# The first expert's gather laced into its first chunk, with its low halves on VectorE and six loads ahead in one ring

## The chip, the cores and the metric

The kernel runs on one core of a Trainium2 chip, in one launch. The metric is the device time in microseconds (us) of that core. PE is TensorE, DVE is VectorE, ACT is ScalarE, POOL is GpSimd and SP is SyncE, whose queue issues the loads of the weights here.

## What is computed

A trunk of two decoder layers on 256 tokens of width 1024, in fp32: latent attention and a dense feed-forward block, then a gated delta rule and a block of 8 experts, of which each token uses two. The part that matters here is the experts':

```python
def moe_ffn(h, w_router, w_gate_up, w_down):
    t = h.reshape(B * S, D)
    logits = (t @ w_router).astype(jnp.float32)
    top_val, top_idx = lax.top_k(logits, TOP_K)
    top_w = jax.nn.softmax(top_val, axis=-1)
    combine = jnp.sum(jax.nn.one_hot(top_idx, N_EXPERTS) * top_w[..., None], axis=1)
    out = jnp.zeros((B * S, D), jnp.float32)
    for e in range(N_EXPERTS):
        y_e = swiglu_ffn(t, w_gate_up[e], w_down[e])   # (silu(gate) * up) @ down
        out = out + combine[:, e:e + 1] * y_e
    return out
```

`w_gate_up` is 1024 by 2 x 1408 for each expert, `w_down` 1408 by 1024. `t` is the normalised and modulated state of the 256 tokens.

## The kernel before

**Halves.** A product in fp32 is made of three products of numbers rounded to fp32r: high by high, low by high, high by low. So each slab of weights is split: ACT casts it to the high half `whi` (L199), and another engine subtracts that from the slab to get the low half `wlo` (L200), here DVE, since `pool_share` is 0 in this phase (L1739). The pool `wsp` has four buffers for each half (L59), so at most four split slabs wait for PE.

**Loads.** `wload` (L182) takes a buffer of 512 KB and issues the load on SP. In the experts' phase `in_turn` (L1734) says which ring the buffer is from: `wr2`, six buffers in memory that the phase before gives up when it ends (L1730), or `wrw`, ten buffers that exist all along (L57). Three loads of eight go to `wr2`. The slabs 0 to 3 of expert 0 are loaded and split in the phase before (`tokens`, L1610) and wait in the list `pre`. The list `ahead` (L1753) holds two more loads, of slabs 4 and 5; `routed` (L1764) splits them.

**Routing and gather.** `routed` makes the two weights of each token (it holds an exponential and a switch of ACT's function table, L1772 and L1773, and four small matmuls, L1778, whose result DVE copies, L1779). `place` (L1841) writes a matrix `P` that picks the tokens of an expert. `gather` (L1871) then, after a row of factors `xr`, makes for each of eight blocks `k` of 128 features: four matmuls with `P` (L1901), DVE's scaling `xg` (L1905), ACT's high half `XH` (L1910), and the low half `XL`. For the first group `share` is true: for odd blocks ACT writes a full-precision copy `full` (L1917) and POOL subtracts (L1918); for even blocks DVE does it in one instruction (L1920), one block late.

**The expert.** `expert` (L2057) goes through chunks of 512, 512 and 384 columns of gate and up. For a chunk of 512 it takes eight slabs (L2064); for each, six matmuls (L2069): high by `XH`, low by `XH`, high by `XL`, for two parts of 256 columns each. After slabs 3, 5 and 7 `sides` (L2051) advances side work. For expert 0 that is `first_sides` (L2119): `turns_of` (L1782, 15 small DVE instructions that find the order of the experts), placements for the next group, `weights_of` (L1803, 17 small DVE instructions and one of ACT), then the next group's gather. After the chunk come the gating (`gated`, L2037), the transposes and halves `ah` and `al` (`turned`, L2007), and, a chunk later, the products with `w_down` (`down`, L1973).

**Order.** Inside `manual_schedule` PE, DVE, ACT and POOL run in the order in which the program is written. Outside, a planner lays out the instructions when the program is built. SP's loads are always laid out by the planner. Before, the written order ends after the whole gather and `routed` (`order.close()`, L2136), ahead of expert 0; its chunks and the side work are the planner's.

Of the kernel before, what the change touches and what calls it, by code (L numbers as in the profile page):

```python
# [8 lines left out]
F32 = mybir.dt.float32  # L9
# [3 lines left out]
AF = mybir.ActivationFunctionType  # L13
# [4 lines left out]
S = 256  # L18
# [31 lines left out]
def hybrid_kernel(ctx: ExitStack, tc: tile.TileContext, rope_rows, x, c, positions, ada_w, ada_b,  # L50
# [1682 lines left out]

    def in_turn():  # L1734
        nload[0] += 1
        return wr2 if nload[0] % 8 in (0, 3, 6) else wrw

    ring.append(in_turn)
    pool_share[0] = 0  # L1739
# [10 lines left out]
    nc.gpsimd.tensor_copy(slot2[:, 0:64], slot[:, 0:64])  # L1750
    nc.gpsimd.tensor_copy(slot2[:, 192:256], slot[:, 0:64])

    ahead = [gu_load(0, k0, 0, 512) for k0 in (4, 5)]  # L1753
    cnt, cntm, trank, eidS, cntS = (sm.tile([128, NE], F32, name=n, bufs=1) for n in ("cnt", "cntm", "trank", "eidS", "cntS"))
    tge, perm = (sm.tile([128, NE, NE], F32, name=n, bufs=1) for n in ("tge", "perm"))
    chosS, posS, w2s = rt("chosS"), rt("posS"), rt("w2s", (128, 2, 1))
# [7 lines left out]
    def routed():  # L1764

        mx, w2 = rt("mx", (128, 2, 2)), rt("w2", (128, 2, 1))
        nc.vector.tensor_scalar(oh0, rank, 1.0, None, op0=OP.is_lt)
        nc.vector.reduce_max(mx[:, :, 0:1], lg, axis=AX.X)
        nc.vector.scalar_tensor_tensor(lg, in0=oh0, scalar=-3e38, in1=lg, op0=OP.mult, op1=OP.add)
        nc.vector.reduce_max(mx[:, :, 1:2], lg, axis=AX.X)  # L1770
        nc.vector.tensor_tensor(w2, mx[:, :, 1:2], mx[:, :, 0:1], op=OP.subtract)
        nc.scalar.activation(w2, w2, AF.Exp)  # L1772
        warm(AF.Silu)  # L1773
        for raw in ahead:
            pre.append(wsplit(raw, [128, 1, 2, 512]))
        pt = acc_bank("tot")
        for t in range(2):
            mm(pt[:, 0:NE], lhsT=ones32[:, 0:1].to_broadcast([128, 128]), rhs=chos[:, t], start=t == 0, stop=t == 1)  # L1778
        nc.vector.tensor_copy(cnt, pt[:, 0:NE])  # L1779
        nc.vector.tensor_copy(w2s, w2)  # L1780
# [47 lines left out]
    def experts(again, between):  # L1828
# [39 lines left out]

        XS = {}

        def gather(g, share=False):  # L1871

            es = gathers[g]
            small = [e for e in es if kinds[e] == "S"]
# [22 lines left out]
            for k in range(8):  # L1897
                ps = mm_bank("xg")
                for j, src in enumerate((xtH, xtL)):
                    for t in range(2):  # L1900
                        mm(ps[:, :n], lhsT=src[:, t, k * 128:(k + 1) * 128], rhs=P[:, t, pl],  # L1901
                           start=j == 0 and t == 0, stop=j == 1 and t == 1)
                xg = sm.tile([128, S], F32, name="xg", tag="xg")
                sh = modT[1, 3][:, k:k + 1]
                nc.vector.scalar_tensor_tensor(xg[:, :n], in0=ps[:, :n], scalar=scl[1, 1][:, k:k + 1], in1=xr[:, :n],  # L1905
                                               op0=OP.mult, op1=OP.mult)
                xb = xg[:, bo:bo + 128]
                while late:
                    late.pop()()
                nc.scalar.activation(XH[:, k, :], xb, AF.Identity, bias=sh)  # L1910
                if small:
                    nc.scalar.activation(XF[:, k, :].rearrange("p (a b) -> p a b", b=64),
                                         xg.rearrange("p (a b) -> p a b", b=64)[:, 0:3 * len(small) - 2:3], AF.Identity,
                                         bias=sh)
                if share and k % 2:
                    full = sm.tile([128, S], F32, name="full", tag="act")
                    nc.scalar.activation(full[:, :128], xb, AF.Identity, bias=sh)  # L1917
                    nc.gpsimd.tensor_tensor(XL[:, k, :], full[:, :128], XH[:, k, :].bitcast(F32), op=OP.subtract)  # L1918
                else:
                    late.append(lambda k=k, xb=xb, sh=sh: nc.vector.scalar_tensor_tensor(  # L1920
                        XL[:, k, :], in0=xb, scalar=sh, in1=XH[:, k, :].bitcast(F32), op0=OP.add, op1=OP.subtract))
                if not share or k == 7:
                    while late:
                        late.pop()()
                yield
# [131 lines left out]
        def expert(e, more):  # L2057
            XH, XL = XS[e]
            for c0, n in groups(e):
# [1 line left out]
                ps = [mm_bank("gu") for _ in parts]  # L2061
                kn = 512 // max(n, 256)
                for k0 in range(0, 8, kn):
                    hi, lo = pre.pop(0) if pre else wsplit(gu_load(e, k0, c0, n), [128, kn, 2, n])  # L2064
                    for k in range(kn):
                        kk = k0 + k
                        for i, (w, x) in enumerate(((hi, XH), (lo, XH), (hi, XL))):
                            for p, (o, m) in zip(ps, parts):
                                mm(p[:, :2 * m].rearrange("p (g c) -> p g c", g=2), lhsT=x[:, kk, :],  # L2069
                                   rhs=w[:, k, :, o:o + m], start=kk == i == 0, stop=kk == 7 and i == 2)  # L2070
                    if k0 % 2 and k0 > 1:
                        sides(more)
                for p, (o, m) in zip(ps, parts):
                    act = sm.tile([128, S], F32, name="act", tag="act", bufs=2)
                    gated((p[:, :m], p[:, m:2 * m]), m, act[:, :m])
# [54 lines left out]
        if again:  # L2130
            list(group(0))
        else:
            place(0, pos, chos)
            list(gather(0, True))
            between()
            order.close()  # L2136
        run = {"B": expert, "S": expert_small}
        for e in range(NE):
            more = [group(g) for g, es in enumerate(gathers) if g and e == es[0] - 1]
# [91 lines left out]
```

## Time and profile before

| what | value |
|---|---|
| median of 3 runs | 995.1 us (992.34 to 997.79) |
| the profiled execution: its own time | 997.03 us |
| the profiled execution: its span | 995.3 us |
| PE busy, share of the span | 931.6 us, 94% |
| DVE busy | 671.4 us, 67% |
| ACT busy | 486.2 us, 49% |
| POOL busy | 123.7 us, 12% |

The span goes from the first to the last instruction of the program in one profiled execution; its time includes what lies around the span. Start times in the views are microseconds from the span's start. The shares are means over stages with different limits; the stage of the change lies between 580 and 655 us. A busy time of PE is modelled, and PE's clock has two levels here, shown as a granted share of 0.50 (1.2 GHz) and 1.00 (2.4 GHz); a value between them is a mean over a stretch.

### The profile page before, as it was taken

The page shows a single profiled execution, that of the slowest core. Times are in us where ns is not written, and L with a number is a line of the kernel's source. Part 1 is how long each engine was busy: PE and PEld are TensorE (multiplying, and loading weights), DVE is VectorE, ACT ScalarE, POOL GpSimd, SP SyncE. Part 2 cuts the span into 40 slices and gives each one's busy share as a digit, 9 for nine tenths or more (in the row PEclk, how much of TensorE's full clock was granted, in tenths as well). Part 3 has the DMA queues.
Part 4 walks back from the last instruction along what each step waited for, and adds up shares of the span by engine and source line. Part 5 has one row for each costly group of instructions (what it writes and reads, how often), then busy time and mean ns, then how long its engine had stood idle before and what let it go on. Part 6 is the DMA issues. An engine that isn't in the chain of part 4 may idle for free. (4 is left out here: it accounts for less than half of the span.)

```text
span 995.3 us, 18930 instructions
## 1 busy us (share of the span) xinstructions
PE 931.6 (94%) x6802; PEld 749.5 (75%) x6802; DVE 671.4 (67%) x1281; ACT 486.2 (49%) x877; POOL 123.7 (12%) x226
## 2 busy tenths in 40 slices
PE   5899999999999999899999989899989999999995
PEld 3787888999999989789889877755774567356642
DVE  5778957877777768977764458925872488257532
ACT  2366646444444457544563366723662366236422
POOL 2000001000000024535663240000000000000000
PEclk7999998999999989899999979999999999999998
DMA  9959995979988955432223365979999999999992
GB/s 308 366 178 315 303 288 167 312 238 338 312 285 293 304 163 179 140 107 86 86 86 101 113 212 175 318 259 370 365 394 370 363 353 342 382 358 367 364 372 71
DMA packets 152741, 261.34 MB, mean 263 GB/s; under 512 B 13650, under 2 KB 104832, under 8 KB 152640
## 3 DMA queue, kind: packets, MB, share of 16 engines
q1 hardware_dynamic: 152336, 259.81, 76.3%
q8 instruction: 55, 0.90, 0.4%
q0 software_dynamic: 304, 0.25, 0.1%
q14 instruction: 46, 0.38, 0.1%
HBM read 258.97 MB, written 1.05 MB: 261 GB/s over the span
## 5 line engine op out<-in xcount | busy, mean ns | idle before, releaser
L463 ACT CAST whi<-w 128x1024 fp32r<-128x1024 f32 (+3 forms) x147 | 138.6, 958 | 115.4 <-PE gu L1145 45.0
L200 DVE TENSOR_TENSOR wlo<-w,whi 128x1024 fp32r<-128x1024 f32 (+1 forms) x136 | 153.0, 1155 | 33.8 <-ACT whi L199 32.1
L468 DVE TENSOR_TENSOR wlo<-w,whi 128x1024 fp32r<-128x1024 f32 (+3 forms) x132 | 147.9, 1135 | 21.6 <-ACT whi L463 21.2
L199 ACT CAST whi<-w 128x1024 fp32r<-128x1024 f32 (+1 forms) x136 | 131.8, 998 | 35.7 <-PE gu L2069 18.5
L1144 PE MATMUL gu<-hhi,whi 128*128 128x256 f32 x336 | 95.4, 284 | 0.0
L1146 PE MATMUL gu<-hhi,wlo 128*128 128x256 f32 x336 | 95.1, 283 | 0.0
L1145 PE MATMUL gu<-hlo,whi 128*128 128x256 f32 x336 | 95.1, 283 | 0.0
L2099 PE MATMUL gu<-w,XF 128*64 128x512 f32 (+1 forms) x384 | 85.3, 564 | 0.0
L232 PE MATMUL pj<-hhi,whi 128*128 128x256 f32 x240 | 73.6, 307 | 0.0
L234 PE MATMUL pj<-hhi,wlo 128*128 128x256 f32 x240 | 68.5, 286 | 3.8 <-DVE wlo L468 3.8
L233 PE MATMUL pj<-hlo,whi 128*128 128x256 f32 x240 | 68.4, 285 | 0.0
L468 POOL TENSOR_TENSOR wlo<-w,whi 128x1024 fp32r<-128x1024 f32 x15 | 39.3, 2622 | 226.3 <-DVE al L1119 181.2
L1145 PEld LDWEIGHTS gu<-hlo,whi 128*128 128x128 f32 x336 | 64.5, 192 | 0.0
L1144 PEld LDWEIGHTS gu<-hhi,whi 128*128 128x128 f32 x336 | 64.5, 192 | 0.0
L1146 PEld LDWEIGHTS gu<-hhi,wlo 128*128 128x128 f32 x336 | 64.5, 192 | 0.0
L2069 PE MATMUL gu<-whi,XH 128*128 128x512 f32 x192 | 59.4, 390 | 3.6 <-ACT whi L199 3.4
L2069 PE MATMUL gu<-wlo,XH 128*128 128x512 f32 x192 | 59.7, 392 | 2.2 <-DVE wlo L200 2.2
L2099 PEld LDWEIGHTS gu<-w,XF 128*64 128x64 f32 x384 | 26.4, 136 | 44.5 <-issue 39.5
L2069 PE MATMUL gu<-whi,XL 128*128 128x512 f32 x192 | 58.2, 385 | 0.0
L262 DVE SCALAR_TENSOR_TENSOR adacc<-adaw,csil,adacc 128x1024 f32<-128x1024 f32 x42 | 56.1, 1336 | 2.2 <-DMA adaw<-in_ada_w_dram 2.2
L1106 PE MATMUL acc<-ah,whi 128*128 128x256 f32 x176 | 50.0, 284 | 0.0
L1107 PE MATMUL acc<-al,whi 128*128 128x256 f32 x176 | 49.8, 283 | 0.0
(526 smaller groups left out, 2213.0 us busy)
## 6 DMA issues: line engine op xcount, KB each, us to landing
w<-in_moe_w_down_dram SPq DMA_DIRECT2D x84, 512.0 KB, 6.8
w<-in_moe_w_gate_up_dram SPq DMA_DIRECT2D x128, 256.0 KB, 5.4
w<-in_moe_w_gate_up_dram SPq DMA_DIRECT2D x64, 512.0 KB, 6.9
adaw<-in_ada_w_dram SPq DMA_DIRECT2D x50, 512.0 KB, 5.3
w<-in_moe_w_gate_up_dram SPq DMA_DIRECT2D x128, 192.0 KB, 4.0
w<-in_ada_w_dram SPq DMA_DIRECT2D x46, 512.0 KB, 6.6
w<-in_ffn_w_gate_up_dram SPq DMA_DIRECT2D x88, 256.0 KB, 5.5
w<-in_gdn_w_in_dram SPq DMA_DIRECT2D x32, 512.0 KB, 4.6
```

The source lines that it names most:

```text
L199: nc.scalar.copy(dv(hi), rv(raw))
L200: eng.tensor_tensor(dv(lo), rv(raw), dv(hi).bitcast(F32), op=OP.subtract)
L232: mm(ps, lhsT=lhi, rhs=rhi, start=first, stop=False)
L233: mm(ps, lhsT=lhi, rhs=rlo, start=False, stop=False)
L234: mm(ps, lhsT=llo, rhs=rhi, start=False, stop=last)
L463: nc.scalar.copy(dv(hi), rv(raw))
L468: eng.tensor_tensor(dv(lo), rv(raw), dv(hi).bitcast(F32), op=OP.subtract)
L1144: mm(o, lhsT=h[:, c], rhs=rh, start=k == g == 0 and new, stop=False, skip_group_check=True)
L1145: mm(o, lhsT=h[:, c], rhs=rl, start=False, stop=False, skip_group_check=True)
L1146: mm(o, lhsT=l[:, c], rhs=rh, start=False, stop=k == 1 and g == 3, skip_group_check=True)
L2069: mm(p[:, :2 * m].rearrange("p (g c) -> p g c", g=2), lhsT=x[:, kk, :], rhs=w[:, k, :, o:o + m], start=kk == i == 0, stop=kk == 7 and i == 2)
L2099: mm(o, lhsT=X[:, k, :], rhs=r, start=k == 0, stop=k == 7, tile_position=(0, 64 * h))
```

## The change

The gather of expert 0 becomes a generator `rows0` that is advanced one block at a time. The factors and the blocks 0 and 1 are made ahead of the expert. In its first chunk a function `step(k)` comes ahead of the products of slab k: it makes block k + 2, at slab 2 it also calls `routed` (`between()`), and at slabs 1 to 6 it splits one of the slabs loaded ahead. The low halves `XL` are all made on DVE, one block late; the branch with `full` and POOL goes. `ahead` holds six loads, slabs 4 to 7 and the first two of the second chunk, and the first six loads all take buffers of `wrw`. `routed` no longer splits. The written order ends after the first chunk's products, so that the side work after slabs 3, 5 and 7 stands in it too.

```diff
--- before.py
+++ after.py
@@ -1733,7 +1733,7 @@
 
     def in_turn():
         nload[0] += 1
-        return wr2 if nload[0] % 8 in (0, 3, 6) else wrw
+        return wr2 if nload[0] > 6 and nload[0] % 8 in (0, 3, 6) else wrw
 
     ring.append(in_turn)
     pool_share[0] = 0
@@ -1750,7 +1750,7 @@
     nc.gpsimd.tensor_copy(slot2[:, 0:64], slot[:, 0:64])
     nc.gpsimd.tensor_copy(slot2[:, 192:256], slot[:, 0:64])
 
-    ahead = [gu_load(0, k0, 0, 512) for k0 in (4, 5)]
+    ahead = [gu_load(0, k0, 0, 512) for k0 in (4, 5, 6, 7)] + [gu_load(0, k0, 512, 512) for k0 in (0, 1)]
     cnt, cntm, trank, eidS, cntS = (sm.tile([128, NE], F32, name=n, bufs=1) for n in ("cnt", "cntm", "trank", "eidS", "cntS"))
     tge, perm = (sm.tile([128, NE, NE], F32, name=n, bufs=1) for n in ("tge", "perm"))
     chosS, posS, w2s = rt("chosS"), rt("posS"), rt("w2s", (128, 2, 1))
@@ -1771,8 +1771,6 @@
         nc.vector.tensor_tensor(w2, mx[:, :, 1:2], mx[:, :, 0:1], op=OP.subtract)
         nc.scalar.activation(w2, w2, AF.Exp)
         warm(AF.Silu)
-        for raw in ahead:
-            pre.append(wsplit(raw, [128, 1, 2, 512]))
         pt = acc_bank("tot")
         for t in range(2):
             mm(pt[:, 0:NE], lhsT=ones32[:, 0:1].to_broadcast([128, 128]), rhs=chos[:, t], start=t == 0, stop=t == 1)
@@ -1868,7 +1866,7 @@
 
         XS = {}
 
-        def gather(g, share=False):
+        def gather(g, late_by=0):
 
             es = gathers[g]
             small = [e for e in es if kinds[e] == "S"]
@@ -1912,14 +1910,9 @@
                     nc.scalar.activation(XF[:, k, :].rearrange("p (a b) -> p a b", b=64),
                                          xg.rearrange("p (a b) -> p a b", b=64)[:, 0:3 * len(small) - 2:3], AF.Identity,
                                          bias=sh)
-                if share and k % 2:
-                    full = sm.tile([128, S], F32, name="full", tag="act")
-                    nc.scalar.activation(full[:, :128], xb, AF.Identity, bias=sh)
-                    nc.gpsimd.tensor_tensor(XL[:, k, :], full[:, :128], XH[:, k, :].bitcast(F32), op=OP.subtract)
-                else:
-                    late.append(lambda k=k, xb=xb, sh=sh: nc.vector.scalar_tensor_tensor(
-                        XL[:, k, :], in0=xb, scalar=sh, in1=XH[:, k, :].bitcast(F32), op0=OP.add, op1=OP.subtract))
-                if not share or k == 7:
+                late.append(lambda k=k, xb=xb, sh=sh: nc.vector.scalar_tensor_tensor(
+                    XL[:, k, :], in0=xb, scalar=sh, in1=XH[:, k, :].bitcast(F32), op0=OP.add, op1=OP.subtract))
+                if not late_by or k == 7:
                     while late:
                         late.pop()()
                 yield
@@ -2061,7 +2054,12 @@
                 ps = [mm_bank("gu") for _ in parts]
                 kn = 512 // max(n, 256)
                 for k0 in range(0, 8, kn):
-                    hi, lo = pre.pop(0) if pre else wsplit(gu_load(e, k0, c0, n), [128, kn, 2, n])
+                    if e == c0 == 0 and not again:
+                        step(k0)
+                    if pre:
+                        hi, lo = pre.pop(0)
+                    else:
+                        hi, lo = wsplit(ahead.pop(0) if ahead else gu_load(e, k0, c0, n), [128, kn, 2, n])
                     for k in range(kn):
                         kk = k0 + k
                         for i, (w, x) in enumerate(((hi, XH), (lo, XH), (hi, XL))):
@@ -2070,6 +2068,8 @@
                                    rhs=w[:, k, :, o:o + m], start=kk == i == 0, stop=kk == 7 and i == 2)
                     if k0 % 2 and k0 > 1:
                         sides(more)
+                if e == c0 == 0 and not again:
+                    order.close()
                 for p, (o, m) in zip(ps, parts):
                     act = sm.tile([128, S], F32, name="act", tag="act", bufs=2)
                     gated((p[:, :m], p[:, m:2 * m]), m, act[:, :m])
@@ -2131,9 +2131,18 @@
             list(group(0))
         else:
             place(0, pos, chos)
-            list(gather(0, True))
-            between()
-            order.close()
+            rows0 = gather(0, 1)
+            for _ in range(3):
+                next(rows0)
+
+            def step(k):
+
+                next(rows0, None)
+                if k == 2:
+                    between()
+                if k > 0 and ahead:
+                    pre.append(wsplit(ahead.pop(0), [128, 1, 2, 512]))
+
         run = {"B": expert, "S": expert_small}
         for e in range(NE):
             more = [group(g) for g, es in enumerate(gathers) if g and e == es[0] - 1]
```

## Rows read from the trace of the kernel before

**Rows 1.** Busy time by stage: us, busy of each engine (instructions), PEclk, DMA, GB/s.

```profile
585.60:594.10 8.50, 8.44 (x40) 8.47 (x40) 3.83 (x13) 3.99 (x12) 1.37 (x3) 0.50 0.91 342
594.20:599.90 5.70, 5.70 (x15) 4.44 (x16) 2.26 (x8) 3.50 (x7) 0.46 (x1) 0.50 0.00 0
608.30:614.40 6.10, 4.73 (x24) 3.70 (x24) 6.10 (x30) 4.38 (x9) 0.00 (x0) 1.00 0.37 118
614.40:632.10 17.70, 17.03 (x83) 13.59 (x83) 17.70 (x34) 11.46 (x21) 0.00 (x0) 1.00 0.85 282
646.30:653.60 7.30, 7.30 (x36) 6.03 (x35) 2.16 (x5) 1.51 (x3) 0.00 (x0) 0.90 0.66 219
```

**Rows 2.** Time line of PE: start, us, instructions merged; gather, then expert 0's first chunk.

```profile
586.54 0.63 PE L1901 MATMUL xg<-P,xtH 128*128 128x128 f32 x2
...
587.40 0.63 PE L1901 MATMUL xg<-P,xtH 128*128 128x128 f32 x2
...
594.18 1.20 PE L2069 MATMUL gu<-whi,XH 128*128 128x512 f32 x2
...
596.89 1.05 PE L2069 MATMUL gu<-whi,XH 128*128 128x512 f32 x2
...
599.45 0.87 PE L2069 MATMUL gu<-whi,XH 128*128 128x512 f32 x2
...
601.08 0.63 PE L2069 MATMUL gu<-whi,XH 128*128 128x512 f32 x2
...
607.62 0.63 PE L2069 MATMUL gu<-whi,XL 128*128 128x512 f32 x2
```

**Rows 3.** Time line of DVE in the same stretch and behind it.

```profile
588.49 0.35 DVE L1905 SCALAR_TENSOR_TENSOR xg<-xg,scl,xr 128x128 f32<-128x128 f32 x1 [0.43 <-PE xg L1901]
...
594.21 0.17 DVE L1767 TENSOR_SCALAR oh<-rank 128x16 f32<-128x16 f32 x1
...
600.77 1.22 DVE L200 TENSOR_TENSOR wlo<-w,whi 128x1024 fp32r<-128x1024 f32 x1 [1.34 <-ACT whi L199]
...
603.51 0.17 DVE L1785 COPY cntm<-cnt 128x8 f32<-128x8 f32 x1
...
610.34 0.27 DVE L1762 TENSOR_REDUCE posS<-byt 128x16 f32<-128x128 f32 x1
...
610.66 1.23 DVE L1845 TENSOR_SCALAR P<-slot,posS,chosS 128x256 fp32r<-128x256 f32 x4
...
614.36 4.61 DVE L200 TENSOR_TENSOR wlo<-w,whi 128x1024 fp32r<-128x1024 f32 x4
```

**Rows 4.** Time line of ACT in the same stretch.

```profile
588.88 0.40 ACT L1910 ACTIVATE XH<-xg,mod 128x128 fp32r<-128x128 f32 x1 [0.38 <-DVE xg L1905]
589.18 0.39 ACT L1917 ACTIVATE full<-xg,mod 128x128 f32<-128x128 f32 x1
...
595.55 1.28 ACT L413 ACT_TABLE_LOAD   x1
...
597.13 1.04 ACT L199 CAST whi<-w 128x1024 fp32r<-128x1024 f32 x1
599.69 1.05 ACT L199 CAST whi<-w 128x1024 fp32r<-128x1024 f32 x1 [1.52 <-PE gu L2069]
```

**Rows 5.** Time line of PE, two of its waits behind the first chunk.

```profile
614.34 0.74 PE L2069 MATMUL gu<-wlo,XH 128*128 128x512 f32 x2 [0.69 <-DVE wlo L200]
...
643.19 0.38 PE L1859 MATMUL psw<-cmb,P 128*128 128x2 f32 x2 [2.65 <-ACT SM L1862]
```

**Rows 6.** Groups of DVE from 600 to 632: count, busy us, mean ns, idle before.

```profile
L1845 DVE TENSOR_SCALAR P<-slot,posS,chosS 128x256 fp32r<-128x256 f32 (+1 forms) x14 | 4.6, 367 | 0.0
...
L2039 DVE TENSOR_TENSOR act<-act,gu 128x256 f32<-128x256 f32 x4 | 1.6, 410 | 0.0
```

**Rows 7.** Time line of SP: loads of gate and up, merged.

```profile
536.56 41.55 SPq L185 DMA_DIRECT2D w<-in_moe_w_gate_up_dram  x20
```

**Rows 8.** Page part 6, DMA issues: count, KB each, median us to landing.

```profile
w<-in_moe_w_gate_up_dram SPq DMA_DIRECT2D x128, 256.0 KB, 5.4
```

## The prediction

> **What bounds the kernel now.** I read the page's busy times first, then a table of busy times by stage, then the time lines of TensorE (PE), VectorE (DVE) and ScalarE (ACT) around the edit. PE is the busiest engine there, so in most places the end is moved by PE's own work or by what makes PE stand still. By stage [rows 1] it looks otherwise around the first expert. While the rows of expert 0 are gathered (585.6 to 594.1) and while its first chunk begins (594.2 to 599.9) PE is full, but at a granted clock of 0.50, 1.2 GHz. Behind 600 it has 1.00. From 608.3 to 614.4 DVE is busy 6.10 of 6.10 us, and from 614.4 to 632.1 17.70 of 17.70: there DVE, not PE, is the scarce engine, and PE waits for it where I follow it: 0.69 us for a low half at 614.34 [rows 5]. Only from 646.3 does DVE have room again (2.16 of 7.30 us). So two questions decide: does PE get through gather and first chunk sooner, and does DVE leave that stretch sooner or later?
>
> **What PE could win.** Before, the gather's eight blocks come first, at half clock 0.86 us each (586.54 to 587.40), and the first product of expert 0 starts at 594.18; a slab's six matmuls take 2.56 us at 1.2 GHz (596.89 to 599.45) and 1.40 us at 2.4 (6.54 us for 14 pairs from 601.08 to 607.62); the last pair, with its 0.63, ends at 608.25 [rows 2]. PE never idles in it. The change sets three blocks ahead of product 0 and puts one block before each of the next five. Product 0 then starts at 586.54 + 3 x 0.86 = 589.1, five microseconds sooner. PE's work is the same, matmul for matmul; the gain is only in the clock. Before, it stayed at 0.50 through 8.5 us of gather and the first 5.8 us of products [rows 1, 2]. If it rises as long after the first product as it did here, or somewhat sooner, that is 593 to 595 instead of 600, and 5 to 7 us at half clock become full ones: 2.5 to 3.5 us of PE time.
>
> **What DVE and ACT must do in each step.** This is the part on the path. In the new first chunk all engines follow the written order. In step k, DVE does xg (block k+2), the low half XL of the block before, then wlo of a slab; ACT does XH of block k+2, then whi of that slab. So wlo waits for whi, whi stands behind XH, XH waits for xg, and the next xg stands behind this wlo: one ring over two engines. Its links: xg to XH 0.39 (588.49 to 588.88), XH to ACT's next 0.30 (588.88 to 589.18), whi to wlo 1.08 (599.69 to 600.77), wlo to DVE's next 1.15 (4.61 for four) [rows 3, 4]. Sum 2.92 us per step. At half clock PE needs 0.86 + 2.56 = 3.42 per step and the ring is hidden; at full clock PE needs half of 0.86 and 1.40 = 1.83 and the ring sets the pace. Before, gather and splits were not laced in one another, and from 600 a split every 1.40 us kept up with PE.
>
> Two things are put into that ring. Step 2 holds `between()`: five small DVE instructions, the exponential, and the switch of ACT's table, all before whi. From the first small one to the whi behind the switch it took 594.21 to 597.13 = 2.92 us [rows 3, 4]. With xg and XL before it (0.27 each by their starts) and wlo's 1.08 + 1.15 behind, step 2 is 5.7 us. The table load in it is 1.28 us by its row, and the cast follows it 0.30 us after its end. The Trainium skill, ScalarE: Activation LUTs, "What ACT_TABLE_LOAD costs", gives each switch a further drain of about 1.38 us, 2.66 in all; the rows here show no such drain ahead of it or behind it, and by that figure, an estimate, the end would be 1.4 us later. The sum does not use it. Step 3 is followed by `turns_of`, 15 DVE instructions of about 0.16 to 0.27 us (first and last in [rows 3]); I take 0.19 each by their starts, 2.8 us. Before, the planner laid them between splits that were already ahead; now wlo of the next slab and XL of the next block are queued behind them, and PE's third pair of each slab waits for that XL.
>
> **The sum.** Block 3 ends at 589.1 + 2.56 + 0.86 = 592.5, its xg starts 0.2 later (588.26 to 588.49), 592.8. Step 1 ends at 595.7, step 2 at 601.4, step 3 with `turns_of` at 607.1, step 4 at 610.0. The last two blocks' low halves: XL of block 6 is ready at 610.6, of block 7 at 611.2 (0.39 + 0.40 + 0.34 behind xg). PE finishes slab 6 at 611.1 and slab 7 at 612.5: 4.2 us after the 608.25 of before, with the clock's gain already spent, since PE waits for XL in slabs 4, 5 and 6. DVE goes on: wlo of slab 8 to 612.9, four placements 1.16 (of the row with 1.23) and seven small ones of `weights_of` at 0.16 to 615.2, wlo of slab 9 to 616.3, ten small ones to 617.9, the two gating products 0.8 [rows 6], wlo of slab 10 by 619.8. Before, that one ended at 614.3, where PE had it [rows 5]. So DVE is 5.5 us late at the point where PE already waited for it.
>
> **Does it come back?** From there to 632 DVE has no idle time in which to catch up, so I let the 5.5 us stand. Downwards, the bound is the placements for later groups, 10 of the 14 that DVE did between 600 and 632 (4.6 us for all, so 3.4 after the first four) [rows 6]: nothing soon needs them, and put off to DVE's room after 646 they would give 3.3 back. Upwards, the bound is the two al subtractions coming ahead of wlo 10 with the wait for their transposes, some 1.4 us more. I take 5.5, since the order of the stage stays as it is written.
>
> **The parts at nothing.** Six loads ahead in the ring of ten: the loads of this chunk were issued from 536 on, and from 594.2 to 599.9 the DMA moved 0 GB/s because no buffer was free [rows 1, 7]. So no split of this stretch waits for a landing, and other buffer turns alone win nothing. What is behind them on SP's queue is freed by wlo 4 to 9, at 596 to 616; the DMA share of 0.37 to 0.85 up to 632 is the cover. If it were gone, one split would wait for one landing, 5.4 us by the page's median [rows 8]. Four low halves move from POOL and ACT to DVE: 4 x 0.27 = 1.1 us, which lie where DVE waits for whi in the ring; without that wait they would cost 1.1. The four `full` activations leave ACT (0.39 each), and were off the path.
>
> **From span to time.** The span of the profiled execution is 995.3 and its time 997.03, 1.9 above the median 995.1 of the runs. With 5.5 more, span 1000.8 and time 1002.5 on its terms; set on the median, 995.1 + 5.5 = **1000.6 us**. Behind 660 PE keeps its pace and loads follow freed buffers, so a shift there passes to the end.
>
> **The rivals.**
> - *The forecast* (0.50): the ring over DVE and ACT, 998.5 to 1004.
> - *Late, but worked off* (0.20): the chunk ends 4 us later, the later placements give way, 5.5 - 3.3 = 2.2 remain: 997.3. For it: DVE's room after 646. Against: these placements stood among urgent splits before, too.
> - *The clock wins* (0.15), on the other side: the low halves run far enough ahead (four buffers) that the ring doesn't hold PE, and PE's 2.5 to 3.5 us reach the end: 992.1. It decides if a step of DVE and ACT stays under 1.83 us at full clock; DVE alone is 0.27 + 0.27 + 1.15 = 1.69, so it needs whi not to wait for xg. For it speaks how long the clock lay at 0.50 while PE was full. The Trainium skill, TensorE: Matmul & The Clock Gate, section "What's actually happening", says "the default state is throttled, and activity releases the throttle"; by that, products laced into the gather release it sooner. The trace agrees that it came back after 5.8 us of products, but 8.5 us of gather before them had not brought it back, and no row tells what a mixture does.
> - *Late and throttled again* (0.15): PE idles about 4 us for XL of block 5 and falls to 0.50, as after the idle 2.65 us at 643.19 [rows 5], behind which the clock is 0.90 on the mean from 646.3 [rows 1]. Slab 7 then takes 2.56 instead of 1.40, the al subtractions come first (1.4): 1003.2 and up to 1006.
> - That the loads do not come sooner at all changes nothing, by the paragraph above.
>
> **The numbers.** Range 994 to 1006: it holds the forecast, the second case, the slow end of the clock case and most of the last one, about 0.8. About 0.5% (5 us) is what a measurement can tell from no change. Slower by more: 0.36 of the forecast's 0.50 and the last case's 0.15, 0.51; faster by more needs more than the clock case gives, 0.05; the rest, 0.44, within.
>
> **What would show it.** Right: in the chunk, wlo to wlo about 2.9 us apart and more in steps 2 and 3, ACT idle for xg, PE idle for XL in slabs 4 to 6, the chunk's last pair near 612, wlo 10 near 620. Clock back by 595. Wrong: no idle PE between 589 and 608 and the chunk done by 605 (the clock case), or a chunk end near 612 and expert 1's first product no later than before (worked off). If DVE's small instructions stand elsewhere than after slab 3, the sum's 2.8 goes.

## The result, and the profile after

The changed kernel takes 1003.3 us in the median of 20 runs (998.46 to 1005.84). The kernel before took 996.5 us in the median of 20 runs beside it (991.68 to 997.79). The ratio is 1.0070, with a 95% interval of 1.0059 to 1.0082: 6.8 us are lost, somewhat more than the 5.5 of the forecast.

The profiled execution of the changed kernel took 1000.44 us, its span 998.7. Its gather begins at 584.93, 0.73 us sooner than in the trace of before, since stages in front of the change ran differently; so stretches are compared by their lengths. First the busy times by stage of the changed kernel: gather and first chunk, then to the first product with `w_down`, then about as far again (us, busy of PE, PEld, DVE, ACT and POOL with instructions, granted clock, DMA share, GB/s).

```profile
584.90:612.60 27.70, 22.22 (x88) 17.50 (x88) 17.65 (x56) 10.97 (x19) 0.00 (x0) 0.71 0.47 164
612.60:629.40 16.80, 15.08 (x78) 12.16 (x78) 15.84 (x38) 10.89 (x19) 0.00 (x0) 1.00 0.64 209
629.40:655.10 25.70, 22.30 (x113) 18.31 (x113) 19.86 (x33) 17.64 (x34) 0.00 (x0) 0.93 0.89 313
```

The same view of the kernel before, with the stages cut at the same instructions:

```profile
585.70:608.20 22.50, 22.50 (x88) 19.36 (x88) 13.19 (x38) 13.85 (x24) 1.82 (x4) 0.68 0.58 200
608.20:624.50 16.30, 14.87 (x78) 12.26 (x78) 16.30 (x44) 10.29 (x20) 0.00 (x0) 1.00 0.67 216
624.50:650.10 25.60, 22.23 (x114) 18.28 (x113) 21.77 (x42) 17.19 (x33) 0.00 (x0) 0.93 0.89 313
```

The loss stands in the first row: the same 88 PE instructions take 27.7 us instead of 22.5, and PE, which was full before, is idle for 5.5 of them. The second stage adds 0.5, the third 0.1. From 655 to 900 us each product starts 4.9 to 5.0 us later than its like before, in both kernels' own times (0.73 of the loss is hidden by the earlier gather). Nothing is worked off up to there. Behind 900 the two executions come nearer, to the 3.4 us by which their spans differ, but not by any work of the change: behind a wait that both have, PE's clock fell in the execution of the kernel before (0.57 on the mean from 900 to 904) and stayed at 1.00 in that of the changed kernel. Before, and after:

```profile
899.99 0.94 PE L2069 MATMUL gu<-whi,XH 128*128 128x512 f32 x2 [1.72 <-ACT whi L199]
```

```profile
904.90 0.73 PE L2067 MATMUL gu<-whi,XH 128*128 128x512 f32 x2 [1.72 <-ACT whi L199]
```

PE's time line of the changed kernel in the chunk (start, us, line and operation, instructions merged, in brackets the wait ahead and what ended it) answers to [rows 2]:

```profile
588.37 1.16 PE L2067 MATMUL gu<-whi,XH 128*128 128x512 f32 x2
...
590.84 0.33 PE L1899 MATMUL xg<-P,xtH 128*128 128x128 f32 x2
...
597.21 0.68 PE L2067 MATMUL gu<-whi,XH 128*128 128x512 f32 x2
...
600.23 0.74 PE L2067 MATMUL gu<-whi,XL 128*128 128x512 f32 x2 [1.88 <-DVE XL L1913]
...
601.50 1.16 PE L2067 MATMUL gu<-whi,XH 128*128 128x512 f32 x2
...
606.95 1.22 PE L2067 MATMUL gu<-whi,XL 128*128 128x512 f32 x2 [3.43 <-DVE XL L1913]
...
611.99 0.63 PE L2067 MATMUL gu<-whi,XL 128*128 128x512 f32 x2
```

Product 0 starts 3.44 us after the gather's start instead of 8.52. The clock is back by 590.84, where a pair of `xg` takes 0.33 instead of 0.63. Then PE waits twice for the low half `XL` of the next block, 1.88 and 3.43 us, which is nearly all of its 5.5 idle. Behind the first wait the clock falls again: at 601.50 a pair of products takes 1.16 instead of 0.68.

The time lines of ACT and of DVE in the same stretch answer to [rows 4] and [rows 3]:

```profile
594.71 0.40 ACT L1908 ACTIVATE XH<-xg,mod 128x128 fp32r<-128x128 f32 x1 [1.55 <-DVE xg L1903]
...
595.96 1.28 ACT L413 ACT_TABLE_LOAD   x1
597.25 0.20 ACT L413 ACTIVATE warmed<-eps_t 128x1 f32<-128x1 f32 x1
597.36 1.03 ACT L199 CAST whi<-w 128x1024 fp32r<-128x1024 f32 x1
599.95 0.40 ACT L1908 ACTIVATE XH<-xg,mod 128x128 fp32r<-128x128 f32 x1 [1.56 <-DVE xg L1903]
...
606.67 0.40 ACT L1908 ACTIVATE XH<-xg,mod 128x128 fp32r<-128x128 f32 x1 [5.38 <-DVE xg L1903]
```

```profile
593.19 1.23 DVE L200 TENSOR_TENSOR wlo<-w,whi 128x1024 fp32r<-128x1024 f32 x1 [1.15 <-ACT whi L199]
594.34 0.34 DVE L1903 SCALAR_TENSOR_TENSOR xg<-xg,scl,xr 128x128 f32<-128x128 f32 x1
...
598.42 1.23 DVE L200 TENSOR_TENSOR wlo<-w,whi 128x1024 fp32r<-128x1024 f32 x1 [2.28 <-ACT whi L199]
599.57 0.34 DVE L1903 SCALAR_TENSOR_TENSOR xg<-xg,scl,xr 128x128 f32<-128x128 f32 x1
...
601.32 1.23 DVE L200 TENSOR_TENSOR wlo<-w,whi 128x1024 fp32r<-128x1024 f32 x1 [1.15 <-ACT whi L199]
602.46 0.16 DVE L1783 COPY cntm<-cnt 128x8 f32<-128x8 f32 x1
...
606.23 0.15 DVE L1798 CAST eidi<-eidS 1x8 int32<-1x8 f32 x1
606.30 0.33 DVE L1903 SCALAR_TENSOR_TENSOR xg<-xg,scl,xr 128x128 f32<-128x128 f32 x1
...
606.82 1.49 DVE L1843 TENSOR_SCALAR P<-slot,posS,chosS 128x128 fp32r<-128x128 f32 x5
608.24 1.21 DVE L200 TENSOR_TENSOR wlo<-w,whi 128x1024 fp32r<-128x1024 f32 x1
...
617.60 1.21 DVE L200 TENSOR_TENSOR wlo<-w,whi 128x1024 fp32r<-128x1024 f32 x1
```

Here the ring is to be seen: DVE waits for `whi` while ACT, ahead of it, had waited for `xg`, each on the other in turn. Of the 5.38 us that ACT waits at 606.67, 3.84 are `turns_of` on DVE, with two placements laid into it (602.46 to 606.30); the rest is the ring's own.

### The profile page after: what moved, and what is told of

Its sections match the earlier page's. It is cut to its first block, busy times and chain, and to the rows that moved or that the text cites. A ratio compares the mean times of both kernels' runs of the same rounds, so it can differ in the third digit from the quotient of the medians.

```text
span 998.7 us, 18930 instructions
## 1 busy us (share of the span) xinstructions
PE 930.3 (93%) x6802; PEld 745.9 (75%) x6802; DVE 672.7 (67%) x1285; ACT 484.4 (48%) x873; POOL 122.3 (12%) x222
## 3 DMA queue, kind: packets, MB, share of 16 engines
HBM read 258.97 MB, written 1.05 MB: 260 GB/s over the span
## 5 line engine op out<-in xcount | busy, mean ns | idle before, releaser
L2067 PE MATMUL gu<-whi,XL 128*128 128x512 f32 x192 | 58.8, 388 | 5.5 <-DVE XL L1913 5.3
```

## The experiments

Two theories stood against each other. The **ring**: DVE and ACT wait for one another in each step, and the switch and `turns_of` make single steps longer. The **load**: DVE simply has more to do ahead of PE in the chunk, in whatever order. A third question was what each of the change's other parts is worth alone. All runs are set against the kernel before, run beside them. The stage is told from the profiled execution, in us from the first matmul of the routing (`pos`, L1720 in all of them), which no version moves:

| kernel | ratio to before, 95% interval | chunk's end | first product with `w_down` | expert 1's first product |
|---|---|---|---|---|
| before | 1 | 23.8 | 40.1 | 69.2 |
| the change | 1.0070 (1.0059 to 1.0082) | 28.9 | 45.7 | 74.9 |
| sides_out | 1.0037 (1.0017 to 1.0056) | 25.6 | 41.9 | 70.3 |
| split_first | 1.0070 (1.0043 to 1.0097) | 29.6 | 44.9 | 72.8 |
| routed_early | 1.0038 (1.0022 to 1.0054) | 28.2 | 44.9 | 74.1 |
| all_three | 1.0019 (0.9999 to 1.0040) | 24.8 | 41.0 | 71.0 |
| low_late | 0.9994 (0.9977 to 1.0011) | 24.8 | 40.8 | 70.6 |
| ring_sides | 1.0025 (1.0014 to 1.0036) | 20.4 | 43.0 | 72.3 |
| open_ring | 0.9959 (0.9943 to 0.9975) | 21.9 | 37.7 | 65.6 |
| loads_only | 0.9995 (0.9977 to 1.0014) | 23.8 | 40.0 | 69.2 |
| lows_only | 1.0032 (1.0017 to 1.0048) | 23.1 | 41.9 | 70.9 |
| routed_first | 0.9993 (0.9980 to 1.0005) | 22.7 | 38.7 | 67.6 |

The last three columns are of single executions, some of them far from their kernel's median: the changed kernel's lies 2.9 us under it, routed_early's 3.9 above (the slowest of 11), split_first's 4.3 under (the fastest of 6). The last column also holds a fall of the clock that no edit aims at, behind PE's wait for `psw` (643.19 in [rows 5]). From that product to expert 1's first it takes 9.3 us in sides_out, split_first and open_ring, where the clock did not fall there, 11.5 and 11.8 in all_three and low_late, where it fell for longest, and 10.3 to 10.4 in the others.

**1. The side work out of the chunk** (sides_out). The changed kernel, with the three advances of the side work behind the written order:

```diff
-                    if k0 % 2 and k0 > 1:
+                    if k0 % 2 and k0 > 1 and (again or e or c0):
                         sides(more)
                 if e == c0 == 0 and not again:
                     order.close()
+                    for _ in range(3):
+                        sides(more)
```

> The changed kernel, but the three calls of side work in the first chunk (the 15 small instructions of turns_of, the placements, weights_of) stand behind the chunk and behind the end of the written order. Ring theory (wlo, whi, XH and xg of one step follow one another over DVE and ACT, and side work and table switch are queued in that ring): PE's wait of 3.43 us for XL in slab 5 goes, the one of 1.88 us in slab 4 stays; the chunk ends about 3 us sooner than the changed kernel's 612.6, near 609.5, and of the 6.8 us lost some 3 come back: 3 to 4 us above before. Rival (DVE's whole work until 632 sets the end, wherever the side work stands): the chunk ends sooner, but the side work comes due right behind it and the time stays 6 to 7 us above before.

About half of the loss goes (1.0037). In the trace the wait in slab 5 shrinks from 3.43 to 0.40 us, and that in slab 4 stays (1.91):

```profile
601.53 0.73 PE L2067 MATMUL gu<-whi,XL 128*128 128x512 f32 x2 [1.91 <-DVE XL L1913]
...
604.48 1.22 PE L2067 MATMUL gu<-whi,XL 128*128 128x512 f32 x2 [0.40 <-DVE XL L1913]
```

So `turns_of` makes the longer wait, and not the shorter. Its instructions are still done in the chunk: the planner laid them into DVE's wait for the switch (596.91 to 599.54).

**2. The split ahead of the next block** (split_first). In `step`, the slab's split comes first and the next block second:

```diff
             def step(k):
 
-                next(rows0, None)
-                if k == 2:
-                    between()
                 if k > 0 and ahead:
                     pre.append(wsplit(ahead.pop(0), [128, 1, 2, 512]))
+                next(rows0, None)
+                if k == 2:
+                    between()
```

> The changed kernel with one order turned round: in each step the slab is split first and the gather's block comes behind it, so that whi no longer stands behind XH. Ring theory: wlo to wlo falls from 2.9 us to what DVE needs by itself, 1.7 to 1.9; the wait in slab 4 goes, the one in slab 5 shrinks to 1 to 2 us since turns_of is still ahead of XL; 2 to 4 us above before. Rival (the small instructions and the table switch alone make PE wait, the order of split and block does not matter): steps 1 and 4 are shorter, but the chunk ends within 1 us of the changed kernel's 612.6 and the time stays 6 to 7 us above before.

What the ring theory expected came in slab 5 alone: PE waits 3.13 us in slab 4 and 1.70 in slab 5, where it had waited 1.88 and 3.43, and 1.0070 is no better than the change. The low halves of slabs 4 and 5 are still 2.90 us apart, as by DVE's line for the second (the first starts at 589.38). ACT's time line shows why:

```profile
593.80 0.40 ACT L1908 ACTIVATE XH<-xg,mod 128x128 fp32r<-128x128 f32 x1 [1.55 <-DVE xg L1903]
...
599.03 0.40 ACT L1908 ACTIVATE XH<-xg,mod 128x128 fp32r<-128x128 f32 x1 [1.55 <-DVE xg L1903]
599.34 1.03 ACT L199 CAST whi<-w 128x1024 fp32r<-128x1024 f32 x1
```

```profile
592.28 1.22 DVE L200 TENSOR_TENSOR wlo<-w,whi 128x1024 fp32r<-128x1024 f32 x1 [1.15 <-ACT whi L199]
```

ACT still waits 1.55 us for `xg` ahead of each `XH`, and `whi` still stands right behind it: turning the two around within a step only makes the ring close over the end of the step. As I had put it, "order in the step" was the wrong lever; what has to go is that `wlo` stands ahead of an `xg` while its own `whi` is still to come.

**3. The routing ahead of the gather** (routed_early):

```diff
+            between()
             rows0 = gather(0, 1)
...
-                if k == 2:
-                    between()
```

> The changed kernel with routed (five small DVE instructions, the exponential, the switch of ACT's table) ahead of the gather, where ACT stands idle, instead of in step 2. Ring theory: step 2 is 2.4 to 2.8 us shorter, the wait in slab 4 goes and the wait in slab 5 ends that much sooner; the chunk ends near 610, the time is 4 us above before. Rival (the table switch is hidden while PE is at half clock): nothing moves, 6 to 7 us above before.

Again about half of the loss goes (1.0038). The wait in slab 4 is gone and slab 5's is 4.01 instead of 3.43:

```profile
606.88 1.22 PE L2067 MATMUL gu<-whi,XL 128*128 128x512 f32 x2 [4.01 <-DVE XL L1913]
```

So the switch, with the routing's small instructions around it, makes the first wait, and `turns_of` the second. The trace shows which wait goes, not what that is worth: DVE's step 2 is 2.89 us (from low half to low half, 595.47 to 598.36) instead of 5.23, but in this slowest of the 11 executions the clock was back only 8.7 us after the gather's start, and the chunk ends 0.7 us sooner than the change's, where the theory had some 2.6. The half of the loss is read from the median.

**4. The three together** (all_three).

> The changed kernel with all three: side work behind the chunk, split ahead of the block in each step, routed ahead of the gather. Ring theory: PE does not wait in the chunk, its clock is back by 595 and stays, the chunk ends at 603 to 605; how much reaches the end depends on DVE, which has the same work to do until 632: between 0 and 4 us below before. Rival (DVE's whole work sets the end): the chunk ends at 605, but the slabs of the second chunk wait for their low halves, and the time is 0 to 3 us above before.

1.0019, and not the gain that was expected. PE still waits four times for `XL`, 0.79 to 1.23 us, once in each of the slabs 3 to 6, with the low halves of slabs 2.9 to 3.1 us apart. The last of them:

```profile
603.85 0.73 PE L2067 MATMUL gu<-whi,XL 128*128 128x512 f32 x2 [1.23 <-DVE XL L1913]
```

With both long steps gone, what is left is the bare ring of the forecast (2.92 us).

**5. The low half one step late** (low_late). The side work and the switch stay where the change put them. Only `wlo` is issued a step after its `whi`, behind the next block's `xg` and `XL`:

```diff
+            lows = []
...
+                while lows:
+                    lows.pop()()
                 if k > 0 and ahead:
-                    pre.append(wsplit(ahead.pop(0), [128, 1, 2, 512]))
+                    raw = ahead.pop(0)
+                    hi, lo = half_tiles([128, 1, 2, 512])
+                    nc.scalar.copy(hi, raw)
+                    lows.append(lambda: nc.vector.tensor_tensor(lo, raw, hi.bitcast(F32), op=OP.subtract))
+                    pre.append((hi, lo))
```

> The changed kernel with each wlo of the first chunk issued one step after its whi, behind the next step's xg and XL; side work and table switch stay in the written order. The order split-then-block did not open the ring, since XH of the step before stands ahead of whi just as well; this does: wlo finds its whi done. Ring theory: DVE's step falls from 2.9 to about 1.7 us, the wait in slab 4 shrinks below 1 us; turns_of still stands ahead of XL of block 5, so a wait of 2 to 3 us in slab 5 stays; 3 to 5 us above before. Rival (side work and table switch alone cost the time, the ring nothing): within 1 us of the changed kernel, 6 to 8 us above before.

This alone takes back the whole loss (0.9994), more than was expected, with no work taken off DVE. That decides for the ring and against the load. DVE's time line, and PE's one wait in the chunk:

```profile
592.98 1.23 DVE L2151 TENSOR_TENSOR wlo<-w,whi 128x1024 fp32r<-128x1024 f32 x1
594.12 0.35 DVE L1903 SCALAR_TENSOR_TENSOR xg<-xg,scl,xr 128x128 f32<-128x128 f32 x1
...
595.35 1.23 DVE L2151 TENSOR_TENSOR wlo<-w,whi 128x1024 fp32r<-128x1024 f32 x1 [0.63 <-ACT whi L2150]
596.50 0.17 DVE L1783 COPY cntm<-cnt 128x8 f32<-128x8 f32 x1
```

```profile
600.99 0.73 PE L2067 MATMUL gu<-whi,XL 128*128 128x512 f32 x2 [2.81 <-DVE XL L1913]
```

The trace has expert 1's first product 1.4 us later than before, but none of it is the chunk's: the 1.0 us by which that ends later is made up by the time of the product for `psw`, which starts 58.8 us after `pos` in both kernels (643.19 in [rows 5]), here behind this wait:

```profile
640.24 0.59 PE L1857 MATMUL psw<-cmb,P 128*128 128x2 f32 x2 [2.79 <-ACT SM L1860]
```

Only behind it the two part: here the clock lay at half for 6.8 us (0.51 on the mean from 640.2 to 647.0), in the execution before for half as long. The switch hardly holds anything any more (0.63 us of DVE at 595.35, none of PE); `turns_of`, from 596.50, still does.

**6. The ring open, and both long steps out** (open_ring): the edits of 1, 3 and 5 together.

> The changed kernel with the ring opened (each wlo one step after its whi), the side work behind the chunk and routed ahead of the gather. Ring theory: no wait of PE above 0.3 us in the first chunk, from the gather's first matmul to the chunk's end 20 to 21 us (before 22.6, the changed kernel 27.7); the time is 1 to 4 us below before. Rival (DVE's whole work until 632 sets the end): the chunk is as short, but the second chunk's slabs wait for their low halves and the time is the one of before, within 2 us.

0.9959: 4.1 us under the kernel before (2.5 to 5.7), the fastest of all. PE waits once in the chunk, 0.40 us, where none above 0.3 was expected, and its clock does not fall again in this stage:

```profile
605.95 0.73 PE L2067 MATMUL gu<-wlo,XH 128*128 128x512 f32 x2 [0.40 <-DVE wlo L2152]
...
641.59 0.38 PE L1857 MATMUL psw<-cmb,P 128*128 128x2 f32 x2 [2.62 <-ACT SM L1860]
```

In the trace 2.4 us of the gain are there at the first product with `w_down`, and 2.5 at the one for `psw`. Of the 3.6 at expert 1's first product the other 1.1 come from the clock, which did not fall behind the wait of 2.62 us in this execution.

**7. The loads alone** (loads_only). The kernel before with the six loads ahead, all of `wrw`; the splits of slabs 4 and 5 stay in `routed`.

> The kernel before with the loads alone changed: six loads ahead, the first six in the ring of ten. All theories: nothing, within 0.3% of before, since no split of the first chunk waited for a landing. Rival (later loads come late, because the buffers of the second chunk and of the down weights take other turns): 1 to 3 us above before, seen as casts that wait for a landing.

Nothing, as expected (0.9995); the stage is the same to 0.1 us.

**8. The low halves alone** (lows_only). The kernel before with all eight `XL` on DVE, without `full` and POOL:

```diff
-                if share and k % 2:
-                    full = sm.tile([128, S], F32, name="full", tag="act")
-                    nc.scalar.activation(full[:, :128], xb, AF.Identity, bias=sh)
-                    nc.gpsimd.tensor_tensor(XL[:, k, :], full[:, :128], XH[:, k, :].bitcast(F32), op=OP.subtract)
-                else:
-                    late.append(lambda k=k, xb=xb, sh=sh: nc.vector.scalar_tensor_tensor(
-                        XL[:, k, :], in0=xb, scalar=sh, in1=XH[:, k, :].bitcast(F32), op0=OP.add, op1=OP.subtract))
+                late.append(lambda k=k, xb=xb, sh=sh: nc.vector.scalar_tensor_tensor(
+                    XL[:, k, :], in0=xb, scalar=sh, in1=XH[:, k, :].bitcast(F32), op0=OP.add, op1=OP.subtract))
```

> The kernel before with the gather's low halves alone changed: all eight on DVE, no copy on ACT, no subtraction on POOL. Ring theory: nothing, within 0.3% of before, since DVE waits 0.2 to 0.6 us for each block of the gather anyway and one more XL takes 0.27. Rival (DVE's work sets the end up to 632, so four more instructions count): 1.1 us above before.

A miss: 1.0032, 3.2 us slower, where nothing was expected. The chunk does not end later (23.1 against 23.8; the clock was back 4.0 us after the first product, where it had taken 5.8 with the same work of PE). The loss comes in the second chunk. PE's time line, and DVE's ahead of it:

```profile
613.76 1.04 PE L2064 MATMUL gu<-wlo,XH 128*128 128x512 f32 x2 [0.92 <-DVE mosti L1825]
```

```profile
606.38 0.42 DVE L2034 TENSOR_TENSOR act<-act,gu 128x256 f32<-128x256 f32 x1 [1.29 <-ACT act L2033]
...
607.40 1.22 DVE L200 TENSOR_TENSOR wlo<-w,whi 128x1024 fp32r<-128x1024 f32 x1
...
612.50 1.21 DVE L200 TENSOR_TENSOR wlo<-w,whi 128x1024 fp32r<-128x1024 f32 x1
```

The planner laid out DVE's work in another order. Before, six low halves stand ahead of the two gating products, here five: DVE is idle for 1.29 us ahead of the first gating product (606.38) and makes slab 9's low half behind both (607.40), and slab 10's starts 29.4 us after `pos` instead of 28.7. At slab 10's second pair PE waits 0.92 us (0.69 before [rows 5]), and here, not before, it then runs at 0.50 for 3.4 us, a pair at 1.04 instead of 0.63. By the table 1.7 to 1.8 us of the loss are in the trace at that point and at expert 1. Whether the clock falls there in each execution, and what the rest of the 3.2 (1.7 to 4.8) is, stays open.

**9. The ring open and the side work out, the switch left in step 2** (ring_sides): the edits of 1 and 5.

> The changed kernel with each low half of a slab issued one step late and the side work behind the chunk; the routing with its table switch stays in step 2. Two theories on what the fully opened version (4.1 us under the kernel before) owes to which part. (A) With the ring open, the wait of 2.81 us at slab 5 that is left when only the low halves are late belongs to turns_of: here it goes, the chunk ends near 20.8 us after the start of the gather (20.3 in the fully opened version, 23.6 with the low halves late alone), the median lies 2 to 3.5 us under the kernel before, and the switch in step 2 costs at most 0.5 us of PE. (B) The switch is next in line: PE waits 1.5 to 2 us for the low half of block 4 or 5, as it did with the side work out alone (1.91), the chunk ends near 22, and the median lies 0 to 2 us under the kernel before.

Theory A is right on the chunk and wrong on the time. The chunk ends 3.4 us sooner than before (19.1 us after the start of the gather, with the clock back 6.1 us after it, not 8.8 as in open_ring), with no wait of PE above 0.3 us in it; yet the run is slower (1.0025), and slower than with the side work left in (0.9994). Behind the chunk, PE and DVE:

```profile
604.08 0.44 PE L2003 MATMUL at<-ident,act 128*128 128x128 f32 x2 [1.62 <-DVE act L2032]
607.56 0.69 PE L2003 MATMUL at<-ident,act 128*128 128x128 f32 x2 [3.05 <-DVE act L2032]
607.90 1.20 PE L2067 MATMUL gu<-whi,XH 128*128 128x512 f32 x2
```

```profile
603.61 0.41 DVE L2032 TENSOR_TENSOR act<-act,gu 128x256 f32<-128x256 f32 x1
...
607.09 0.41 DVE L2032 TENSOR_TENSOR act<-act,gu 128x256 f32<-128x256 f32 x1
```

The first gating product stands behind three low halves in a row and two small instructions (599.98 to 603.61), and PE waits 1.62 us for it. Between the two gating products stand another 17 instructions of side work and placements, 3.15 us (603.94 to 607.09); PE waits 3.05 us for the second, and the clock falls to 0.50 for 6.8 us. All that the chunk had gained, and 2.9 us more, is gone at the first product with `w_down` (43.0 against 40.1).

In open_ring, DVE's time line shows where the same work went:

```profile
587.54 0.17 DVE L1783 COPY cntm<-cnt 128x8 f32<-128x8 f32 x1
...
592.49 0.15 DVE L1798 CAST eidi<-eidS 1x8 int32<-1x8 f32 x1
...
608.09 0.73 DVE L2032 TENSOR_TENSOR act<-act,gu 128x256 f32<-128x256 f32 x2
```

With the routing ahead of the gather its counts are there at 587.5, and the planner, free to move the side work, laid `turns_of` into the gather, where PE runs at half clock and DVE has room (3.83 busy of 8.50 us in [rows 1]). Nothing of it is left between the gating products at 608.09.

**10. The routing first, without the lacing** (routed_first). The kernel before, with `between()` ahead of the gather and the splits of slabs 4 and 5 behind it.

> The kernel before, its gather not laced, with the routing ahead of the gather and the splits of slabs 4 and 5 behind the gather. It asks whether the gain of the fully opened version is due to the earlier routing alone. If the gain is that of PE's clock in the laced chunk, then here nothing is won: PE was full from 586.5 to 608.3 in the kernel before, so the chunk ends 22.6 us after the start of the gather as there, the clock comes back after the start of the products as there, and the median is 0 to 1.5 us above the kernel before (the gather stands behind the routing). If the table switch ahead of the splits was what cost the kernel before its time, the median is 2 to 4 us under it.

0.9993 (0.9980 to 1.0005): nothing that could be measured, as the first theory expected, though the trace has expert 1's first product 1.6 us sooner. Here too the planner laid `turns_of` into the gather (its first instruction starts at 585.50). So the gain of open_ring isn't that of the early routing alone, nor that of `turns_of` in the gather: its interval (0.9943 to 0.9975) lies below this one, though only just, and in the traces it is another 1.0 us ahead at the first product with `w_down` (the 2.0 at expert 1's first product hold a fall of the clock behind `psw` that open_ring's execution did not have). What it has besides is the lacing with its loads and low halves, and of these neither the loads nor the low halves won anything alone.

## Why the prediction came out as it did

**The ring: right.** The steps of the sum, against the rows above, with 0.73 added for the earlier gather: step 1 was to end at 595.7 and ends at 595.1 (594.34 + 0.73); step 2 at 601.4, and ends at 600.3 (599.57); step 3 with `turns_of` at 607.1, and ends at 607.0 (606.30). The marks named for it are there: low halves 5.23 and then 2.90 us apart (593.19, 598.42, 601.32), ACT idle for `xg`, PE idle for `XL` in slabs 4 and 5, though hardly in slab 6. Step 3 without `turns_of` took 2.89 us (599.57 to 602.46) for the 2.92 of the four links. The chunk's end was to be 612.5 and is 613.3 (611.99 + 0.63 + 0.73); slab 10's low half was to be ready by 619.8 and is at 619.5 (617.60 + 1.15 + 0.73). Experiment 4 showed the ring bare, and experiment 5 that opening it is enough.

**`turns_of`: mis-sized.** I took 2.8 us; it took 3.84 from its first instruction to the next `xg`. Two placements for later groups (0.33 us each by their starts) had been laid between its instructions, and the 15 themselves took some 3.2. The sum came out all the same, by luck in this part: two other terms were 1.1 us too long, since the clock was back sooner (step 1 ended 0.6 sooner) and step 2 took 5.23 us and not 5.7.

**PE's gain: the direction right, the size wrong twice.** The clock was back by 590.84, sooner than the 593 to 595 of the sum: within 2.5 us of the first product, not 5.8 as before [rows 2]. The 5.8 was one execution's; where gather and products aren't laced either, it took 5.6 us (loads_only), 4.0 (lows_only) and 4.4 (routed_first). Then it fell again behind the wait of 1.88 us, from 600.9 to 611.1. The rival "late and throttled again" had this, at a wrong place and price: it let slab 7 run at half clock, and slab 7 ran at full. While the clock was down the ring set the pace anyway (PE waits 3.43 us in that stretch), so the second throttling cost less than the rival gave it: some 0.5 us in slab 6, whose last pair runs from 610.02 to 611.04, most of the 0.8 by which the chunk ended behind the sum. With products laced in, the clock was back 5.7 to 8.8 us after the gather's start in the eight laced kernels, against 12.2 to 14.3 in the four others. The Trainium skill, TensorE: Matmul & The Clock Gate, section "What's actually happening", on which the rival "the clock wins" leaned, says that activity releases the throttle; the traces agree for the products laced in, but the gather alone had kept PE busy too (8.44 of 8.50 us [rows 1]) and had not released it. That rival needed `whi` not to wait for `xg`; in the change it did wait, each time, and with the ring open it no longer held PE: there the chunk ends 20.3 us (open_ring) and 19.1 us (ring_sides) after the gather's start instead of 22.6, 2.3 and 3.5 sooner, about the 2.5 to 3.5 that were forecast as PE's gain. What of open_ring's 4.1 at the end is the clock's isn't separated.

**The table switch: right.** The row is 1.28 us (595.96), and the cast behind `warmed` starts at 597.36, 0.12 after the load's end. The Trainium skill, ScalarE: Activation LUTs, section "What ACT_TABLE_LOAD costs", adds a drain; no row shows one here, and the measurement decides.

**What is late stays late: right.** Of the second case, "late but worked off", nothing came. The placements for later groups weren't put off but drawn forward: ten of the 14 stand in the chunk (for one, five at 606.82, ahead of a `wlo` that had little more than its `whi` to wait for). They emptied DVE somewhat behind the chunk (15.84 busy of 16.80 us, not 16.30 of 16.30 as before in the same stage), but that stage was 0.5 us longer, not shorter.

**The parts at nothing.** The loads: right, by experiment 7. The four low halves: right in the changed kernel, where each `XL` lies ahead of a wait of 1.15 us or more for `whi`; but as an edit of their own they cost 3.2 us, as far as the trace shows by an order of the planner's that no row of before could have told. The price of nothing held for the place, not for the edit.

**The sum.** Predicted +5.5, measured +6.8 (5.9 to 8.2). The profiled pair has +5.1 at the chunk's end (27.7 against 22.6 us from the gather's start), +5.6 at the first product with `w_down` and +5.7 at expert 1's first product; at the end it has +3.4, by the fall of the clock near 900 in the kernel before. So the forecast's mechanism and place are right, and its sum is right to 0.2 us at expert 1 in this pair, with errors in it that cancel; that the median lost about 1 us more isn't located: single executions scatter by more (the changed kernel's 20 runs spread over 7.4 us).

## What to carry to other kernels

When two engines that run in order pass two streams to each other, put the half that needs the other engine's answer one step behind: here the same instructions, with `wlo` one step late, took back the whole loss of 6.8 us. Before work is laced into a tight stretch, look for the stretch where the engine has room and ask what must be known for it to go there: the small instructions cost 3 us between gating products and nothing in the gather, once the routing stood ahead of it. A stage that ends sooner proves nothing: ring_sides ended its chunk 3.4 us sooner and the run was slower.

## What the runs showed of the hardware

The gather alone, with PE busy 8.44 of 8.50 us, had not brought the clock back [rows 1]. With products laced in behind the third block, it was back 5.7 us after the gather's start in the change and 8.8 us in open_ring (595.64, a pair at 0.68); in the four kernels without the lacing it took 12.2 to 14.3 us. The clock fell again behind single waits of PE, such as 1.88 us in the change and 2.81 us in low_late, with a loss in the rows that follow (a pair at 1.05 to 1.16 instead of 0.63 to 0.68). It did not fall behind each of them: it stayed at 1.00 behind 1.76 us in sides_out (611.47) and 1.70 us in all_three (607.69). Behind two waits that every version here has, 1.72 us near 900 and some 2.6 us for `psw`, it fell in some executions and not in others, which alone makes 1 to 2.5 us between two traces.
